# The output side of a SwiGLU on one core: where the low parts, the residual tiles and the last additions are made

## The chip, the cores and the metric

The kernel runs on one core of a Trainium2 chip. The metric is the device time of one execution in microseconds (us); the time given for a kernel is the median of its runs. The core's engines work side by side, each through a queue of its own, in order: TensorE (PE, with its weight loads PEld), VectorE (DVE), ScalarE (ACT), GpSimd (POOL) and SyncE (SP), which issues all DMAs of this kernel.

## The reference

One layer of a decoder trunk with 2048 tokens and 1024 channels, in float32. What matters here is its end:

```python
h = x * (1.0 + sc2) + sh2
gate, up = jnp.split(h @ w_ffn_in[l], 2, axis=-1)
f = (jax.nn.silu(gate) * up) @ w_ffn_out[l]
x = layer_norm(DEEPNORM_ALPHA * x + (1.0 + gt2) * f, ln2_g[l], ln2_b[l])
```

`w_ffn_out` has 2816 rows and 1024 columns. Ahead of this lie the input projection, a short convolution, an RWKV-7 time mixing and the output projection of the mixer with its own norm, which the change doesn't touch.

## The kernel before

Every large product is made in three matmuls of float32r operands: a float32 operand is split into a high part (a cast on ACT, line 232) and a low part (raw minus high, line 233, on an engine that the caller names), and TensorE adds high x high, low x high and high x low (lines 236 to 238, `mm3`). The two products of the SwiGLU also use the scheme with seven block products instead of eight (`PRODS`): the operands of a block product are sums or differences of blocks, made on DVE (line 988), then split.

The output side, the subject here, runs through 72 **steps**: seven products, each over 11 slices k of the hidden dimension. In the first six products a step serves both halves of the tokens: 2 halves x 4 tiles of 128 tokens x 3 matmuls, 24 of them. The last product is done for one half and then for the other, 12 matmuls a step. A product's eight PSUM banks (all that there are) collect over its 11 slices. Then `gather` (line 1007, DVE; copies on ACT in two products) adds each bank into the result tiles `c`, and the next product's first matmul on a bank waits for that.

`operands` makes what a step needs. For each half a tile `fr` is loaded (line 1235, four buffers), cast to `fh` on ACT and reduced to `fl` on DVE. For the weights one or two blocks `w` are loaded (line 1246), combined into `ws` on DVE (line 988, one buffer for even and one for odd k), cast to `oh` on ACT, and the low part `ol` is made by the engine that line 1274 passes to `combine`. The program asks for the operands of a step two steps ahead of its matmuls. The buffers (16 for `fh` and `fl`, four each for `oh` and `ol`) hold those of four steps.

Two more kinds of work go on beside the steps. `residuals` makes 32 tiles `r` of alpha * (normed x * g + b): a load of 128 x 512 values (line 1191) into buffers that the input side's operands used before, then a multiplication (line 1192) and an addition (line 1193). Sixteen are asked for in every second step of the first three products, the other sixteen one by one, each when `added` (line 1203, DVE) has used one up. `after` puts `added`, the statistics (line 1210, DVE) and `norm` into a list `later`, from which `do_later` takes one or two entries a step. `norm` works on a token tile: mean and variance (DVE), the root (POOL, lines 291 and 292), a scalar on DVE (line 293), then for each half row a scaling on ACT (line 1219), a multiplication on DVE (line 1220), an addition (line 1222; on DVE for the last four of 32, on POOL for the others) and the store.

The order on TensorE is the program's. On the other engines and on SP a planner sets the order: it keeps the program's order as priority, and in its own model of the time takes what is ready. So an engine's queue is fixed before the run, and on the chip an instruction whose input is late holds all behind it.

Of the kernel before, what the change touches and what calls it, by code (L numbers as in the profile page):

```python
# [14 lines left out]
ALU = mybir.AluOpType  # L15
# [7 lines left out]
S = 2048  # L23
# [10 lines left out]
HT = 1024  # L34
# [85 lines left out]
def kernel(  # L120
# [21 lines left out]
    act, dve, pool, pe = nc.scalar, nc.vector, nc.gpsimd, nc.tensor  # L142
# [87 lines left out]
    def split(hi, lo, raw, lo_eng=None):  # L230

        act.copy(out=hi, in_=raw)  # L232
        (lo_eng or pool).tensor_sub(lo, raw, hi)  # L233
# [13 lines left out]
    def f512(tag, name, bufs, dt=F32):  # L247
        return wp.tile([P, 512], dt, tag=tag, name=name, bufs=bufs)
# [38 lines left out]
    def norm_scale(st, u):  # L287
        mv = lnp.tile([P, 2], F32, tag="mv", name="mv" + u, bufs=2)
        dve.bn_aggr(out=mv, in_=st)
        rs = lnp.tile([P, 2], F32, tag="rs", name="rs" + u, bufs=2)  # L290
        pool.tensor_scalar(rs[:, 0:1], mv[:, 1:2], LN_EPS, None, ALU.add)
        pool.tensor_tensor(out=rs[:, 0:1], in0=rs[:, 0:1], in1=nhalf[:, 0:1], op=ALU.pow)  # L292
        dve.scalar_tensor_tensor(out=rs[:, 1:2], in0=mv[:, 0:1], scalar=-1.0, in1=rs[:, 0:1],  # L293
                                 op0=ALU.mult, op1=ALU.mult)
        return rs
# [9 lines left out]
    def out_proj(q, spawn, raws=None):  # L305
# [51 lines left out]
        for ns in ((0, 1), (2,), (3,), (4,), (5,), (6, 7)):  # L357
# [6 lines left out]
            for n, ps in zip(ns, pss):  # L364
                mt = lnp.tile([P, QT], F32, tag="mt", name=f"mt{q}_{n}", bufs=1)
                act.activation(mt, ps, AF.Identity, scale=gt1p[:, n:n + 1])
                spawn(add(n, mt))
        spawn(norm(), True)


# [614 lines left out]
    def plus_minus(out, blocks, terms, eng=None):  # L985

        a, b = terms
        (eng or dve).tensor_tensor(out=out, in0=blocks[a], in1=blocks[b.lstrip("-")],  # L988
                                   op=ALU.subtract if b[0] == "-" else ALU.add)

    def combine(blocks, terms, hi, lo, out, lo_eng):

        if len(terms) == 1:
            t = blocks[terms[0]]
        else:
            t = out()
            plus_minus(t, blocks, terms)
        split(hi, lo, t, lo_eng)
        return hi, lo
# [34 lines left out]
    with ExitStack() as ph2:  # L1034
# [128 lines left out]
        rw3 = []  # L1163
# [21 lines left out]
        def residuals():  # L1185

            for n, (b, half, t) in enumerate((b, half, t) for b in ("12", "11", "22", "21") for half in range(2)
                                             for t in range(4)):
                t0, ms = half * HT + (int(b[0]) - 1) * 512 + t * P, slice((int(b[1]) - 1) * 512, int(b[1]) * 512)
                r = fa.tile([P, 512], F32, tag=("h22", "h26")[n % 2], name=f"r{half}_{b}_{t}", bufs=8)  # L1190
                load(out=r, in_=xhd[t0:t0 + P, ms])
                pool.tensor_tensor(out=r, in0=r, in1=rw3[1][:, ms], op=ALU.mult)
                pool.tensor_tensor(out=r, in0=r, in1=rw3[2][:, ms], op=ALU.add)
                rs_made.append(r)
                yield

        stats = {}

        rs_made, rs_todo = collections.deque(), residuals()

        def added(half, b, t):
# [10 lines left out]
        def norm(c, half, a, t):  # L1212

            t0 = half * HT + (int(a) - 1) * 512 + t * P
            rs = norm_scale(stats[half, a, t], f"b{half}_{a}_{t}")
            for m in range(2):
                ms = slice(m * 512, (m + 1) * 512)
                z = c.pop((f"{a}{m + 1}", t))
                act.activation(z, z, AF.Identity, scale=rs[:, 0:1], bias=rs[:, 1:2])  # L1219
                dve.tensor_tensor(out=z, in0=z, in1=rw3[3][:, ms], op=ALU.mult)  # L1220
                end = m and half == S // HT - 1 and a == "2"
                (dve if end else pool).tensor_tensor(out=z, in0=z, in1=rw3[4][:, ms], op=ALU.add)  # L1222
                load(out=out[0, t0:t0 + P, ms], in_=z)


# [4 lines left out]
        def f_loads():  # L1230
            for halves, p, k in steps:
                i = PRODS[p][0]
                for half in halves:
                    f = fa.tile([P, 512], F32, tag="rawx", name=f"fr{half}_{i}_{k}", bufs=4)
                    load(out=f, in_=fd[half, i - 1, k])
                    yield f

        def w_loads():
            for halves, p, k in steps:
                if halves[0]:  # L1240
                    return
                blocks = {}
                for b in (b.lstrip("-") for b in PRODS[p][2]):
                    blocks[b] = fa.tile([P, 512], F32, tag="h25", name=f"w{p}_{b}_{k}", bufs=8)
                    ms = slice((int(b[1]) - 1) * 512, int(b[1]) * 512)
                    load(out=blocks[b], in_=wfs[FK * (int(b[0]) - 1) + k, :, ms])
                yield blocks

        def operands():
            fs, ws, blocks, kept = f_loads(), w_loads(), [], []  # L1250
            got = list(itertools.islice(fs, 2))
            for n, (halves, p, k) in enumerate(steps):
                i, _, terms = PRODS[p]
                F = {}
                for half in halves:
                    got += itertools.islice(fs, 1)
                    F[half] = [fa.tile([P, 512], F32R, tag=("h23", "h21")[n % 2], name=f"f{x}{half}_{i}_{k}", bufs=8)
                               for x in "hl"]
                    split(*F[half], got.pop(0), dve)
                if halves[0]:  # L1260
                    yield F, *kept.pop(0)
                    continue
                u = f"{i}_{k}"
                t = None
                if len(terms) == 2:
                    t = (lnp.tile([P, 512], F32, tag="mt", name="ws" + u, bufs=1) if k % 2 else
                         fa.tile([P, 512], F32, tag="us", name="ws" + u, bufs=1))
                if p == 6 and k < 8:
                    wh, wl = (fa.tile([P, 512], F32R, tag=tag, name=f"o{x}{u}", bufs=8)
                              for x, tag in (("h", "h22"), ("l", "h26")))  # L1270
                else:
                    wh, wl = (f512("w" + x, f"o{x}{u}", 4, F32R) for x in "hl")
                blocks += itertools.islice(ws, 3 - len(blocks))
                w = combine(blocks.pop(0), terms, wh, wl, lambda: t, pool)
                if p == 6:
                    kept.append(w)
                yield F, *w

        with tc.manual_schedule(engines={mybir.EngineType.PE}):
            todo3, got3 = operands(), []  # L1280

            run(ffn_in())
# [3 lines left out]
        def after(half, i, t):  # L1286

            then = {
                1: ((added, half, "12", t), (stat, c[half], half, "12", t)),
                4: ((added, half, "21", t),),  # L1290
                7: ((stat, c[half], half, "11", t), (norm, c[half], half, "1", t)),
                2: ((stat, c[half], half, "21", t),),
                6: ((stat, c[half], half, "22", t), (norm, c[half], half, "2", t)),
            }.get(i, ())
            return [functools.partial(*f) for f in then]
# [120 lines left out]
```

## Time and profile before

| | us |
|---|---|
| median of 3 runs | 2925.76 |
| lowest and highest run | 2925.40, 2932.94 |
| the profiled execution's own time | 2924.91 |
| its span, first to last instruction | 2922.7 |
| busy in the span: PE, DVE, ACT, POOL | 2680.6, 1921.0, 1095.7, 1412.7 |
| the output side: its first matmul, its last one | 2420.8, 2909.0 |

All rows come from the profiled execution. Times in a timeline are from the start of its span. A row that groups instructions gives line, engine, operation, output tile and inputs, the count, the busy time, the mean duration in ns, and then the idle time of that engine just ahead of them with what ended it. The stretches of a table by stretches were cut at the output side's matmuls: each time 264 of them (132 for the two parts of the last product) are one product. In such a table "PEclk" is the granted share of TensorE's full clock, 1.00 for 2.4 GHz and 0.50 for 1.2 GHz.

### The profile page before, as it was taken

The page shows a single profiled execution, that of the slowest core. Times are in us where ns is not written, and L with a number is a line of the kernel's source. Part 1 is how long each engine was busy: PE and PEld are TensorE (multiplying, and loading weights), DVE is VectorE, ACT ScalarE, POOL GpSimd, SP SyncE. Part 2 cuts the span into 40 slices and gives each one's busy share as a digit, 9 for nine tenths or more (in the row PEclk, how much of TensorE's full clock was granted, in tenths as well). Part 3 has the DMA queues.
Part 4 walks back from the last instruction along what each step waited for, and adds up shares of the span by engine and source line. Part 5 has one row for each costly group of instructions (what it writes and reads, how often), then busy time and mean ns, then how long its engine had stood idle before and what let it go on. Part 6 is the DMA issues. An engine that isn't in the chain of part 4 may idle for free. (4 is left out here: it accounts for less than half of the span.)

```text
span 2922.7 us, 50258 instructions
## 1 busy us (share of the span) xinstructions
PE 2680.6 (92%) x19232; PEld 2095.8 (72%) x19232; DVE 1921.0 (66%) x2964; ACT 1095.7 (37%) x1995; POOL 1412.7 (48%) x1104
## 2 busy tenths in 40 slices
PE   7879999999999999988599999988899998997998
PEld 6667777777777777767377888856678887776776
DVE  7354655556455565554674777798897778359597
ACT  4553433335433433434444433333233333332342
POOL 4665333323433333323544444458884448338383
PEclk7898999989999999999699999989999999998999
DMA  6443322234322222324353532235653337555563
GB/s 238 140 130 112 89 64 69 73 99 133 108 64 83 69 67 70 92 75 148 111 176 127 162 101 97 91 101 184 221 189 106 106 107 263 157 187 158 175 214 108
DMA packets 248344, 369.86 MB, mean 127 GB/s; under 512 B 58660, under 2 KB 81188, under 8 KB 248104
## 3 DMA queue, kind: packets, MB, share of 16 engines
q1 hardware_dynamic: 248104, 366.65, 39.5%
q8 instruction: 151, 2.47, 0.4%
q14 instruction: 89, 0.73, 0.1%
HBM read 278.99 MB, written 87.56 MB: 125 GB/s over the span
## 5 line engine op out<-in xcount | busy, mean ns | idle before, releaser
L236 PE MATMUL f<-uh,wh 128*128 128x512 f32 x1232 | 497.8, 404 | 31.9 <-ACT uh L232 27.4
L238 PE MATMUL f<-uh,wl 128*128 128x512 f32 x1232 | 496.2, 403 | 18.1 <-POOL wl L233 18.0
L237 PE MATMUL f<-ul,wh 128*128 128x512 f32 x1232 | 495.5, 402 | 11.8 <-DVE ul L233 7.2
L233 POOL TENSOR_TENSOR l<-r,h 128x512 fp32r<-128x512 f32 x201 | 265.6, 1324 | 438.4 <-ACT h L232 352.2
L233 POOL TENSOR_TENSOR wl<-ws,wh 128x512 fp32r<-128x512 f32 x220 | 316.1, 1438 | 295.5 <-ACT wh L232 264.1
L236 PEld LDWEIGHTS f<-uh,wh 128*128 128x128 f32 x1232 | 235.3, 191 | 92.6 <-ACT uh L232 31.8
L238 PEld LDWEIGHTS f<-uh,wl 128*128 128x128 f32 x1232 | 235.9, 191 | 83.4 <-POOL wl L233 27.9
L988 DVE TENSOR_TENSOR ws<-w,w 128x512 f32<-128x512 f32 x275 | 264.4, 984 | 43.6 <-POOL ol L233 24.6
L237 PEld LDWEIGHTS f<-ul,wh 128*128 128x128 f32 x1232 | 236.0, 192 | 72.4 <-DVE ul L233 9.4
L232 ACT CAST wh<-ws 128x512 fp32r<-128x512 f32 x220 | 136.7, 621 | 363.4 <-DVE ws L988 252.8
L236 PE MATMUL o<-oh,fh 128*128 128x512 f32 x616 | 249.5, 405 | 23.3 <-DVE c L1007 15.1
L1007 DVE TENSOR_TENSOR c<-f,c 128x512 f32<-128x512 f32 x264 | 181.1, 686 | 124.0 <-PE f L238 67.2
L237 PE MATMUL o<-ol,fh 128*128 128x512 f32 x616 | 247.9, 402 | 11.0 <-POOL ol L233 11.0
L238 PE MATMUL o<-oh,fl 128*128 128x512 f32 x616 | 247.8, 402 | 6.6 <-DVE fl L233 6.6
L233 DVE TENSOR_TENSOR fl<-fr,fh 128x512 fp32r<-128x512 f32 x154 | 149.7, 984 | 98.5 <-ACT fh L232 85.0
L232 ACT CAST h<-r 128x512 fp32r<-128x512 f32 x201 | 123.5, 616 | 214.3 <-PE d L270 156.7
L232 ACT CAST fh<-fr 128x512 fp32r<-128x512 f32 x154 | 94.9, 620 | 229.9 <-PE o L237 134.8
L233 POOL TENSOR_TENSOR lo<-ro,ho 128x512 fp32r<-128x512 f32 x64 | 84.7, 1328 | 199.1 <-ACT ho L232 144.3
L236 PEld LDWEIGHTS o<-oh,fh 128*128 128x128 f32 x616 | 119.4, 194 | 53.8 <-DVE c L1007 19.1
L233 POOL TENSOR_TENSOR wl<-w,wh 128x512 fp32r<-128x512 f32 x88 | 126.4, 1436 | 49.9 <-ACT wh L232 49.9
L237 PEld LDWEIGHTS o<-ol,fh 128*128 128x128 f32 x616 | 119.4, 194 | 40.7 <-POOL ol L233 14.4
L238 PEld LDWEIGHTS o<-oh,fl 128*128 128x128 f32 x616 | 119.4, 194 | 35.3 <-DVE fl L233 8.2
(499 smaller groups left out, 5898.2 us busy)
## 6 DMA issues: line engine op xcount, KB each, us to landing
r<-in_win_dram SPq DMA_DIRECT2D x201, 256.0 KB
w<-in_wfi_dram SPq DMA_DIRECT2D x176, 256.0 KB
fr<-fd SPq DMA_DIRECT2D x154, 256.0 KB
w<-wfs SPq DMA_DIRECT2D x132, 256.0 KB
fd<-fs SPq DMA_DIRECT2D x110, 256.0 KB
wm<-in_wmod_dram SPq DMA_DIRECT2D x72, 256.0 KB
ro<-in_wout_dram SPq DMA_DIRECT2D x64, 256.0 KB
fd<-th SPq DMA_DIRECT2D x44, 256.0 KB
```

Source lines behind the costliest of these rows:

```text
L232: act.copy(out=hi, in_=raw)
L233: (lo_eng or pool).tensor_sub(lo, raw, hi)
L236: pe.matmul(ps, lh, rh, start=start, stop=False)
L237: pe.matmul(ps, lh, rl, start=False, stop=False)
L238: pe.matmul(ps, ll, rh, start=False, stop=stop)
L988: (eng or dve).tensor_tensor(out=out, in0=blocks[a], in1=blocks[b.lstrip("-")], op=ALU.subtract if b[0] == "-" else ALU.add)
L1007: dve.tensor_tensor(out=c[b, t], in0=in0, in1=in1, op=op)
```

## The change

Three kinds of instruction go from POOL to DVE, all on the output side; nothing else is altered. They are the low parts `ol` of the weights (line 1274, 77 instructions), the two operations on each residual tile (lines 1192 and 1193, 64 instructions), and the addition that ends the norm (line 1222, 28 of 32, the other four being on DVE already). POOL keeps the two small operations of the norm's root (lines 291 and 292), and on the input side what it had.

```diff
@@ residuals
-                pool.tensor_tensor(out=r, in0=r, in1=rw3[1][:, ms], op=ALU.mult)
-                pool.tensor_tensor(out=r, in0=r, in1=rw3[2][:, ms], op=ALU.add)
+                dve.tensor_tensor(out=r, in0=r, in1=rw3[1][:, ms], op=ALU.mult)
+                dve.tensor_tensor(out=r, in0=r, in1=rw3[2][:, ms], op=ALU.add)
@@ norm
-                end = m and half == S // HT - 1 and a == "2"
-                (dve if end else pool).tensor_tensor(out=z, in0=z, in1=rw3[4][:, ms], op=ALU.add)
+                dve.tensor_tensor(out=z, in0=z, in1=rw3[4][:, ms], op=ALU.add)
@@ operands
-                w = combine(blocks.pop(0), terms, wh, wl, lambda: t, pool)
+                w = combine(blocks.pop(0), terms, wh, wl, lambda: t, dve)
```

## Rows read from the trace of the kernel before

**Rows 1.** The page's busy times: share of the span, number of instructions.

```profile
PE 2680.6 (92%) x19232; PEld 2095.8 (72%) x19232; DVE 1921.0 (66%) x2964; ACT 1095.7 (37%) x1995; POOL 1412.7 (48%) x1104
```

**Rows 2.** Busy time by stretches: products one to six, the last one's parts, the tail.

```profile
core 0: us, PE busy (x) PEld busy (x) DVE busy (x) ACT busy (x) POOL busy (x), PEclk, DMA share, GB/s
2420.82:2502.19 81.37, 67.44 (x275) 53.46 (x274) 62.77 (x45) 24.03 (x44) 70.17 (x45) 0.92 0.67 216
2502.19:2562.62 60.43, 60.43 (x266) 49.59 (x264) 22.94 (x34) 19.86 (x35) 15.30 (x11) 1.00 0.56 170
2562.62:2623.05 60.43, 60.43 (x266) 49.59 (x265) 31.96 (x47) 19.31 (x34) 16.80 (x12) 1.00 0.64 199
2623.05:2710.88 87.83, 69.84 (x266) 53.80 (x265) 84.97 (x77) 21.47 (x39) 70.32 (x43) 0.86 0.54 169
2710.88:2776.34 65.46, 63.52 (x265) 50.84 (x264) 34.17 (x55) 23.62 (x42) 20.56 (x19) 0.97 0.51 158
2776.34:2846.71 70.37, 65.02 (x265) 51.61 (x264) 66.14 (x68) 30.93 (x53) 59.15 (x44) 0.95 0.71 223
2846.71:2879.04 32.33, 30.67 (x134) 24.55 (x132) 24.05 (x42) 7.80 (x14) 2.27 (x4) 1.00 0.37 106
2879.04:2909.41 30.37, 30.37 (x133) 24.60 (x131) 25.57 (x38) 10.96 (x16) 21.25 (x21) 1.00 0.27 96
2909.41:2922.70 13.29, 0.00 (x1) 0.00 (x0) 8.31 (x12) 3.04 (x4) 4.79 (x5) 0.65 0.32 118
sum 501.88, PE 447.71 PEld 358.03 DVE 360.87 ACT 161.04 POOL 280.61; mean PE 49.75 PEld 39.78 DVE 40.10 ACT 17.89 POOL 31.18
```

**Rows 3.** POOL's groups of instructions by line on the output side.

```profile
L233 POOL TENSOR_TENSOR ol<-ws,oh 128x512 fp32r<-128x512 f32 x55 | 80.9, 1474 | 117.8 <-ACT oh L232 113.5 <-DMA fr<-fd 4.3
L1192 POOL TENSOR_TENSOR r<-r,rws 128x512 f32<-128x512 f32 x32 | 55.6, 1756 | 6.3 <-DMA r<-xhd 6.3
L1193 POOL TENSOR_TENSOR r<-r,rws 128x512 f32<-128x512 f32 x32 | 53.4, 1678 | 0.0
L1222 POOL TENSOR_TENSOR c<-c,b2r 128x512 f32<-128x512 f32 x28 | 43.0, 1549 | 9.4 <-DVE c L1220 9.4
L233 POOL TENSOR_TENSOR ol<-w,oh 128x512 fp32r<-128x512 f32 x22 | 32.6, 1485 | 44.7 <-ACT oh L232 44.7
```

**Rows 4.** DVE's low parts in the quiet stretch 2502 to 2613.

```profile
L233 DVE TENSOR_TENSOR fl<-fr,fh 128x512 fp32r<-128x512 f32 x42 | 30.2, 720 | 51.4 <-ACT fh L232 42.3 <-PE o L237 7.0 <-DMA w<-wfs 2.1
```

**Rows 5.** The same instructions in the crowded stretch 2424 to 2491.

```profile
L233 DVE TENSOR_TENSOR fl<-fr,fh 128x512 fp32r<-128x512 f32 x19 | 31.9, 1723 | 0.0
```

**Rows 6.** DVE's timeline (start, us): POOL idle in the first two rows, busy after.

```profile
2617.46 0.68 DVE L1007 TENSOR_TENSOR c<-o,c 128x512 f32<-128x512 f32 x1
2618.06 0.67 DVE L1007 TENSOR_TENSOR c<-c,c 128x512 f32<-128x512 f32 x1
...
2634.14 1.77 DVE L233 TENSOR_TENSOR fl<-fr,fh 128x512 fp32r<-128x512 f32 x1
2635.83 1.77 DVE L1203 TENSOR_TENSOR c<-c,r 128x512 f32<-128x512 f32 x1
```

**Rows 7.** What TensorE waited for, 2400 to the end: us, times, longest us.

```profile
PE o L236 <- DVE c L1007: 15.1, 8, 4.7
PE o L237 <- POOL ol L233: 11.0, 7, 4.8
PE o L236 <- ACT oh L232: 8.2, 2, 6.1
PE o L238 <- DVE fl L233: 6.6, 3, 3.7
```

**Rows 8.** One load's time to landing, in the chain that ended last.

```profile
2793.45 3.29 DMA fr<-fd
```

**Rows 9.** The last two additions of the norm, in the timeline.

```profile
2917.12 1.74 POOL L1222 TENSOR_TENSOR c<-c,b2r 128x512 f32<-128x512 f32 x1 [1.85 <-DVE c L1220]
2917.78 1.63 DVE L1222 TENSOR_TENSOR c<-c,b2r 128x512 f32<-128x512 f32 x1
```

## Prediction

> **What bounds the kernel now.** I first read the page's busy times: PE is busy for 92% of the span, DVE for 66%, POOL for 48% [rows 1]. That says TensorE sets the time, but not where it loses any. So I cut the output side into its products, 264 matmuls each, and read busy times for each stretch [rows 2]. The second and the third product show what TensorE can do: 60.43 us, PE busy throughout, the clock at 1.00. That is 0.229 us a matmul and 60.43 / 11 = 5.49 us a step. Against it the first product takes 81.4 us, the fourth 87.8, the fifth 65.5, the sixth 70.4, and the first part of the last 32.3 instead of 30.2. In the first product 9 of the 275 matmuls belong to the input side (others count 266), 9 x 0.229 = 2.1 us. The excess is then 21.0 - 2.1 = 18.9, 27.4, 5.0, 9.9 and 2.1 us: **63.3 us** in all, and part of it is the clock, granted at 0.92, 0.86, 0.97 and 0.95 in those four products.
>
> The bad products are those in which POOL is busy: 70.2, 70.3 and 59.2 us in the first, fourth and sixth, 15 to 21 in the others. What TensorE waits for there [rows 7] is the gathering of a bank on DVE (15.1 us), `ol` from POOL (11.0), `oh` (8.2, the cast behind a late `ws`) and `fl` from DVE (6.6). Together they are 40.9 us; the other 22 us of the excess are the lower clock around the stalls and short gaps.
>
> Why are they late? The same instruction, `fl` on DVE, takes 0.72 us in the quiet stretch and 1.72 us in the crowded one [rows 4, 5]. The timeline shows the cause as far as a timeline can: while POOL stands idle, DVE starts an instruction every 0.60 us; while POOL works on SBUF tiles, DVE's with two SBUF inputs start 1.69 us apart [rows 6], and POOL's mean is 1.47 to 1.76 us [rows 3]. Side by side the two engines finish two instructions in about 1.7 us. DVE by itself finishes two in 1.2 us. So a second engine adds no throughput here; it takes some.
>
> **The change, part by part.** 77 `ol`, 64 residual operations and 28 additions leave POOL, 169 instructions that cost it 80.9 + 32.6 + 55.6 + 53.4 + 43.0 = 265.5 us [rows 3]. On DVE I price one at the pitch with POOL idle, 0.60 us [rows 6]: 101 us. No row shows these three operations on DVE alone, but `fl` is the same subtraction on the same shape; its mean of 0.72 us [rows 4], which has some shared ones in it, is the upper price, 122 us. In return DVE's own instructions fall from up to 1.7 us to 0.6. I count what each product then asks of DVE: the instructions of both engines, less the tiny ones of the norm, times 0.60, against TensorE's 60.4 us [rows 2]:
> - first product: 45 + 45 = 90, 54 us
> - second and third: 45 and 59, 27 and 35 us
> - fourth: 77 + 43 = 120, 72 us
> - fifth: 74 less 12 tiny ones, 37 us
> - sixth: 112 less 20 tiny ones, 55 us
> - last: 105 less some 28 tiny ones, 46 us
>
> Only the fourth asks more than it has, by 12 us. Operands may be made up to three steps ahead, 16 us, and the fifth product has 60.4 - 37 = 23 us to spare, so a delay of 12 us of `added` and residual work can be put off, as far as the queue's order puts it behind the operands. The program asks for a step's operands ahead of that step's `later` entries, which speaks for it.
>
> What is late next, product by product, with what I leave of each excess:
> - First, 18.9: the last gathers of the input side hold the first banks and end when the last matmul of that side allows; 17 instructions at 0.6 us in their way instead of 13 at up to 1.8. The stalls on `ol` near its end go. I leave 6 (2 to 11), a gain of **13** (8 to 17).
> - Fourth, 27.4: DVE's 72 us stay above TensorE's. With full cover nothing is left, with none 12 and a clock dip. I leave 5 (0 to 13), a gain of **22.5** (14 to 27).
> - Fifth, 5.0: the wait at its end for a gather and a clock dip. A gain of **3.5** (1 to 5).
> - Sixth, 9.9: here each step gets a `norm` entry, five full DVE instructions beside the four of the operands, 9 x 0.60 = 5.4 us against 5.49. That is tight. A gain of **6** (1 to 9).
> - Last, 2.1: a gain of **1** (0 to 2).
> - Tail of 13.3 us [rows 2]: the last two additions, 1.74 and 1.63 us side by side [rows 9], become two of 0.6 us in turn; against that, DVE has one or two more instructions ahead of the last gather. **0.5** (-1 to +1).
>
> The second and the third product lose nothing, since 27 and 35 us of DVE work in 60.4 leave room; without that room each `ol` would come 0.6 us later per instruction ahead of it. DVE's queue gets two new waits: `ol` behind ACT's cast, and line 1192 behind the load of `r`. Queued behind them are `fl`, `ws` and the gathers, and TensorE waits for those. POOL waited only once for a load of `r`, 6.3 us of 32 loads [rows 3]. The first I price at nothing, because the planner can put another instruction into the 0.6 us of the cast; without that cover it is 77 x 0.6 = 46 us of DVE time, spread over products that mostly have it. SP's queue loses its waits for POOL and gets as many for DVE; its order around them may change, and I price that at nothing, between -2 and +2 us.
>
> Two rules speak against this sum. POOL is busy for 48% of the span and DVE for 66% [rows 1], so work goes from the emptier engine to the fuller one. The Trainium skill, *Perfetto Trace Analysis*, "Identifying the Most-Contended Engine", takes occupancy as a fair measure of how close Vector and GPSIMD are to their limits. By it DVE would be overfilled; that is the third rival. And DVE's starts lie 0.60 us apart although an instruction is shown for 0.67 to 0.68 us [rows 6]. The Trainium skill, *VectorE: DVE Perf Modes*, "The DRAIN you can't avoid", has the next one start only when the pipeline is empty. By 0.68 us a start the fourth product would ask 82 us of DVE instead of 72, and the whole would come out some 10 us later; the row decides.
>
> **The sum.** 13 + 22.5 + 3.5 + 6 + 1 + 0.5 = 46.5 us. The profiled execution's time is 2924.9 us (span 2922.7), 0.9 below the median of the runs, so the sum holds for both: 2925.8 - 46.5 = **2879 us**. The best ends add up to 61 us, the worst to 23: 2865 to 2903 us.
>
> **Rivals.**
> 1. *DVE becomes the bound in its crowded products.* The planner puts residual or norm work ahead of operands, and one queue now carries everything. Then the first product keeps 12 of its excess, the fourth 20, the sixth all: a gain of 6.9 + 7.4 + 3.5 + 1 = 19 us, **2907 us**. For it speaks the fourth product's 72 us, against it the look-ahead of 16 us. Chance 0.12.
> 2. *Slower, through the loads of the residual tiles.* In DVE's queue line 1192 waits for its landing and everything behind it waits too. If each of the 32 waits for w, the first product asks 54 + 16w of DVE and the fourth 72 + 16w. With what the other parts gain (11), the change is even at 18.9 + 27.4 + 11 = (54 + 16w - 60.4) + (72 + 16w - 60.4), w = 1.6 us. At a whole landing time of 3.3 us [rows 8] it loses 32 x (3.3 - 1.6) = 54 us, **2980 us**. Against it: one wait in 32 on POOL [rows 3], whose queue ran late. Chance 0.04.
> 3. *The durations go along.* If 1.5 to 1.7 us were the price of the work itself, DVE would need 361 + 265 = 626 us in a stretch of 502 [rows 2, 3]: 124 us more, **3050 us**. The 0.60 us starts speak against it [rows 6]. Chance 0.01.
> 4. *All stalls go*, more than 61 us gained: about **2862 us**. Every product would run like the second. Chance 0.05.
>
> The change could also fail to do what it says, if the planner's other order on ACT and SP cancels it; that is within the first rival.
>
> **How the numbers follow.** My forecast of 2865 to 2903 has a chance of 0.78. For 8 in 10 the range goes to 2864 and to 2906, into the first rival. Some 0.3%, or 9 us, is what a measurement of this kernel can tell from no change. All of the forecast and of rival 4 is faster by more, and 0.08 of the 0.12 of rival 1: 0.91. Rival 1 leaves 0.04 within it. Slower is 0.05, rivals 2 and 3.
>
> **What would show it.** Every `fl`, `ws`, `ol` and `r` on DVE should have a mean near 0.65 us on the output side, and DVE's busy time there should not rise above its 361 us although it has 169 instructions more. The first and the fourth product should take 62 to 75 us, with the clock near 1.00. The second and the third should stay at 60.4. The forecast is wrong if DVE's instructions stay above 1 us with POOL idle, if DVE shows idle time ended by the load of `r`, or if TensorE waits for `fl` or the gathers as long as now.

## The result and the profile after

| | before | after |
|---|---|---|
| median of 4 runs, us | 2925.58 | 2879.55 |
| lowest and highest run | 2924.19, 2932.94 | 2877.66, 2885.85 |
| the profiled execution's own time | 2924.91 | 2881.27 |
| its span | 2922.7 | 2879.5 |
| output side, first matmul to last | 488.6 | 444.8 |
| from there to the end | 13.3 | 11.5 |

The ratio of the times is 0.9847, with a 95% interval of 0.9834 to 0.9861: 46.0 us less by the medians, 41 to 49 by the interval (0.0139 and 0.0166 of 2925.6), where 46.5 were forecast.

First the table by stretches, cut at the same matmuls as [rows 2]: products one to six, the two parts of the last, the tail.

```profile
2423.20:2491.23 68.03, 64.95 (x276) 52.47 (x274) 55.78 (x92) 26.41 (x47) 0.47 (x1) 0.97 0.77 264
2491.23:2551.66 60.43, 60.43 (x266) 49.58 (x265) 28.85 (x45) 19.80 (x35) 0.00 (x0) 1.00 0.54 170
2551.66:2612.09 60.43, 60.43 (x266) 49.59 (x265) 36.58 (x58) 19.30 (x34) 0.00 (x0) 1.00 0.65 199
2612.09:2686.22 74.13, 64.26 (x266) 51.27 (x265) 73.58 (x123) 23.42 (x41) 0.00 (x0) 0.95 0.64 207
2686.22:2746.76 60.54, 60.54 (x266) 49.50 (x264) 37.13 (x64) 22.86 (x39) 2.89 (x6) 1.00 0.52 166
2746.76:2807.59 60.83, 60.73 (x266) 49.50 (x264) 59.13 (x109) 32.34 (x54) 6.10 (x10) 1.00 0.77 260
2807.59:2837.64 30.05, 30.05 (x134) 24.79 (x133) 20.77 (x37) 7.27 (x13) 1.00 (x3) 1.00 0.35 105
2837.64:2868.01 30.37, 30.36 (x133) 24.58 (x131) 24.07 (x49) 11.35 (x17) 6.42 (x12) 1.00 0.27 96
2868.01:2879.50 11.49, 0.00 (x0) 0.00 (x0) 6.61 (x13) 2.67 (x4) 1.02 (x2) 0.66 0.37 137
sum 456.30, PE 431.75 PEld 351.29 DVE 342.52 ACT 165.43 POOL 17.90; mean PE 47.97 PEld 39.03 DVE 38.06 ACT 18.38 POOL 1.99
```

The columns are those of [rows 2]. Products five and six and the last one now run at TensorE's own pace, the clock at 1.00. The first went from 81.4 to 68.0 us, the fourth from 87.8 to 74.1: these two are what is left. The sum row has the surprise that was forecast: DVE is busy for 342.5 us, less than the 360.9 before, with 169 instructions more. By product the gains are 13.3, 13.7, 4.9, 9.5 and 2.3 us, and 1.8 in the tail, 45.6 in all (the differences to [rows 2]; 0.1 is rounding). The output side began at 2423.2, not 2420.8, so the profiled spans differ by 43.2 only.

That start is not the change's doing. The order of work on DVE and ACT up to there is the same, and the 2.4 us are there already at the first matmul of the SwiGLU's input product (1405.6 us before, 1408.7 after). Among the profiled executions of this study with an unaltered input side that matmul lies between 1398.7 and 1408.7 us, and the output side's first one between 2413.5 and 2423.2. So below I compare the length of the output side, or of one product, and take whole times only as medians.

DVE's groups on the output side, answering to [rows 3 to 5] (L1221 is line 1222 of the kernel before):

```profile
L233 DVE TENSOR_TENSOR fl<-fr,fh 128x512 fp32r<-128x512 f32 x150 | 103.6, 693 | 94.1 <-ACT fh L232 85.8 <-PE o L237 8.2
L233 DVE TENSOR_TENSOR ol<-ws,oh 128x512 fp32r<-128x512 f32 x55 | 38.5, 705 | 0.7 <-ACT oh L232 0.7
L1193 DVE TENSOR_TENSOR r<-r,rws 128x512 f32<-128x512 f32 x32 | 21.7, 705 | 0.0
L1192 DVE TENSOR_TENSOR r<-r,rws 128x512 f32<-128x512 f32 x32 | 21.6, 700 | 0.0
L1221 DVE TENSOR_TENSOR c<-c,b2r 128x512 f32<-128x512 f32 x28 | 19.1, 688 | 0.0
```

Each moved instruction is shown for about 0.70 us, and so is `fl`, crowded or not. Ahead of the residual operations DVE never sat idle for a load: their idle time is 0.0. What TensorE still waits for, answering to [rows 7]:

```profile
PE o L237 <- DVE ol L233: 8.9, 4, 6.1
PE o L236 <- DVE c L1007: 4.1, 2, 2.4
```

13.0 us instead of 40.9. The longest wait, 6.1 us in the fourth product, is for an `ol`, and DVE's timeline shows why it was late (x2 and x3 are two and three in a row):

```profile
2644.40 0.70 DVE L988 TENSOR_TENSOR ws<-w,w 128x512 f32<-128x512 f32 x1
2644.99 0.71 DVE L233 TENSOR_TENSOR fl<-fr,fh 128x512 fp32r<-128x512 f32 x1
2645.59 1.32 DVE L1192 TENSOR_TENSOR r<-r,rws 128x512 f32<-128x512 f32 x2
2646.80 0.71 DVE L988 TENSOR_TENSOR ws<-w,w 128x512 f32<-128x512 f32 x1
2647.40 1.31 DVE L1203 TENSOR_TENSOR c<-c,r 128x512 f32<-128x512 f32 x2
2648.61 0.71 DVE L233 TENSOR_TENSOR fl<-fr,fh 128x512 fp32r<-128x512 f32 x1
2649.21 0.71 DVE L1203 TENSOR_TENSOR c<-c,r 128x512 f32<-128x512 f32 x1
2649.81 1.31 DVE L1193 TENSOR_TENSOR r<-r,rws 128x512 f32<-128x512 f32 x2
2651.01 0.71 DVE L233 TENSOR_TENSOR fl<-fr,fh 128x512 fp32r<-128x512 f32 x1
2651.62 1.91 DVE L1203 TENSOR_TENSOR c<-c,r 128x512 f32<-128x512 f32 x3
2653.42 0.71 DVE L233 TENSOR_TENSOR ol<-ws,oh 128x512 fp32r<-128x512 f32 x1
```

Starts are 0.60 us apart, without a gap. Between the first `ws` and its `ol`, nine microseconds later, stand ten instructions of residual work.

### The profile page after: what moved, and what is told of

It is laid out like the page before. It is cut to its first block, busy times and chain, and to the rows that moved or that the text cites. A ratio compares the mean times of both kernels' runs of the same rounds, so it can differ in the third digit from the quotient of the medians.

```text
span 2879.5 us, 50206 instructions
## 1 busy us (share of the span) xinstructions
PE 2660.8 (92%) x19232; PEld 2082.8 (72%) x19232; DVE 1898.7 (66%) x3133; ACT 1098.7 (38%) x1995; POOL 1148.7 (40%) x935
## 4 chain that ended last, share of the span: by engine, by line
PE 40%; DVE 5%; DMA 4%; POOL 2%; issue 1%; ACT 0%; SPq 0%; POOLq 0%; DVEq 0%; ACTq 0%
PE f L238 8%; PE f L237 8%; PE f L236 8%; PE o L237 4%; PE o L238 4%; PE o L236 4%; PE do L270 3%; DMA wf<-in_wfo_dram 2%; DMA wfs<-wf 2%; POOL wf L1172 1%; DVE c L1007 1%; DVE ws L988 1%; DMA b<-h2d 0%; DVE ul L233 0%; POOL wl L233 0%
## 5 line engine op out<-in xcount | busy, mean ns | idle before, releaser
L233 POOL TENSOR_TENSOR l<-r,h 128x512 fp32r<-128x512 f32 x201 | 265.2, 1321 | 444.8 <-ACT h L232 359.5
L238 PEld LDWEIGHTS f<-uh,wl 128*128 128x128 f32 x1232 | 234.8, 191 | 85.6 <-POOL wl L233 30.5
L988 DVE TENSOR_TENSOR ws<-w,w 128x512 f32<-128x512 f32 x275 | 242.8, 907 | 18.0 <-DMA w<-wfs 7.4
L236 PE MATMUL o<-oh,fh 128*128 128x512 f32 x616 | 242.1, 393 | 4.2 <-DVE c L1007 4.1
L233 DVE TENSOR_TENSOR fl<-fr,fh 128x512 fp32r<-128x512 f32 x154 | 106.2, 693 | 94.1 <-ACT fh L232 85.8
```

The source lines that it names most:

```text
L236: pe.matmul(ps, lh, rh, start=start, stop=False)
L238: pe.matmul(ps, ll, rh, start=False, stop=stop)
```

## The experiments

Theory A: an instruction of DVE with two SBUF inputs and one of POOL slow each other down, so what counts is how long both work side by side. Theory B: DVE's pace does not matter; a moved instruction takes 0.7 us instead of 1.5, and `ol` leaves POOL's queue. A second question is what the fourth product still loses.

### One part of the change alone

Three kernels each make one of the three edits of the change and leave out the other two.

```diff
 only_residuals
-                pool.tensor_tensor(out=r, in0=r, in1=rw3[1][:, ms], op=ALU.mult)
-                pool.tensor_tensor(out=r, in0=r, in1=rw3[2][:, ms], op=ALU.add)
+                dve.tensor_tensor(out=r, in0=r, in1=rw3[1][:, ms], op=ALU.mult)
+                dve.tensor_tensor(out=r, in0=r, in1=rw3[2][:, ms], op=ALU.add)
 only_low_parts
-                w = combine(blocks.pop(0), terms, wh, wl, lambda: t, pool)
+                w = combine(blocks.pop(0), terms, wh, wl, lambda: t, dve)
 only_norm_add
-                (dve if end else pool).tensor_tensor(out=z, in0=z, in1=rw3[4][:, ms], op=ALU.add)
+                dve.tensor_tensor(out=z, in0=z, in1=rw3[4][:, ms], op=ALU.add)
```

> Of the change only the 64 residual operations go to DVE; the low parts ol and the last additions of the norm stay on POOL. Theory A (an instruction of DVE with two SBUF inputs and one of POOL slow each other down, so what counts is how long both work side by side): the residual work is POOL's long stretch in products one and four, so most of their gain comes by it alone: 22 to 32 us faster than before (2894 to 2904 us), product six as slow as before (about 70 us), fl on DVE near 0.75 us in the first product. Theory B (the gain is that a moved instruction takes 0.7 us instead of 1.5 and ol leaves POOL's queue; DVE's own pace does not matter): residual tiles were never waited for, so only ol's freer queue on POOL helps, 11 us of waits: 5 to 12 us faster (2914 to 2921 us).

> Of the change only the 77 low parts ol go to DVE; residual tiles and norm additions stay on POOL. Theory A: POOL still works for 109 us on residual tiles beside DVE, now with more instructions on the slowed DVE: between 8 us faster and 8 us slower than before (2918 to 2934 us); product four stays above 82 us, fl in it above 1.1 us. Theory B: ol no longer queues behind residual tiles and takes half as long, so the 11 us of waits for it and the clock behind them come back: 15 to 30 us faster (2896 to 2911 us).

> Of the change only the 28 additions that end the norm go to DVE. Theory A: product six, where POOL made 14 of them, falls from 70.4 to 61 to 65 us and the tail loses 1 to 2 us; products one and four as before: 6 to 11 us faster (2915 to 2920 us). Theory B: nobody on TensorE waits for these additions, only the stores do; 0 to 2 us faster, all of it in the tail (2924 to 2926 us).

Measured: 2895.73 us with the residual operations alone (ratio to before 0.9911, 0.9894 to 0.9927), 2908.70 with the low parts alone (0.9952, 0.9937 to 0.9967), 2917.68 with the norm's additions alone (0.9979, 0.9968 to 0.9990). The output sides are 458.1, 473.5 and 483.0 us long, 30.5, 15.1 and 5.6 less than before. The parts add up to 51.2 us, all together gave 43.8, so they share some of it.

The tables by stretches, each with products one, four and six: first the residual operations alone, then the low parts alone, then the additions alone.

```profile
2418.79:2488.70 69.91, 65.81 (x275) 53.13 (x274) 56.19 (x78) 24.33 (x44) 29.39 (x13) 0.95 0.76 254
2609.55:2679.22 69.67, 63.81 (x265) 51.47 (x264) 68.51 (x105) 23.10 (x40) 28.05 (x11) 0.95 0.63 198
...
2743.13:2814.83 71.70, 65.05 (x265) 51.12 (x264) 67.68 (x70) 31.54 (x54) 59.25 (x44) 0.95 0.69 220
```

```profile
2422.51:2496.55 74.04, 67.27 (x276) 53.35 (x275) 67.80 (x57) 23.08 (x43) 56.56 (x32) 0.95 0.70 234
2617.40:2710.31 92.91, 66.60 (x266) 52.68 (x265) 86.12 (x96) 23.63 (x41) 48.63 (x31) 0.83 0.52 167
...
2770.73:2832.87 62.14, 60.99 (x266) 49.43 (x265) 60.32 (x87) 31.86 (x54) 31.39 (x26) 1.00 0.75 249
```

```profile
2422.14:2503.71 81.57, 67.60 (x275) 53.69 (x274) 62.77 (x45) 24.58 (x45) 70.20 (x45) 0.92 0.66 216
2624.57:2712.36 87.79, 69.65 (x266) 53.67 (x264) 84.71 (x75) 21.00 (x37) 69.84 (x43) 0.86 0.53 169
...
2777.52:2844.67 67.15, 63.27 (x266) 50.53 (x265) 62.83 (x88) 31.61 (x54) 40.23 (x29) 0.97 0.74 235
```

The residual operations came out as A had them and B had not, product six no faster at 71.7 us; only `fl` in the first product, 0.83 us in the mean, stayed above the 0.75 expected. The low parts did not: A's 2918 to 2934 us missed, B's 2896 to 2911 held. In the fourth product A was right: with POOL still 48.6 us on residual tiles it got worse, 87.8 to 92.9 us, since `ol` now waits in the slowed queue (TensorE waited for it once for 17.1 us); `fl` there has a mean of 0.95 us, not the 1.1 expected. What I had not counted is that `ol` leaves POOL also in the first and the sixth product, where that shortens the time side by side (POOL 70.2 to 56.6 and 59.2 to 31.4 us); they gained 7.3 and 8.2 us. The norm's additions brought the forecast total, but product six only fell to 67.2, not to 65: POOL still made 19 `ol` there. These three do not tell A from B cleanly.

### POOL busy again, for nobody

The changed kernel, and beside each residual tile POOL works on a scratch tile that nobody else reads. The two kernels differ in what POOL does: in the first it reads SBUF, in the second it only writes. The lines that set up the two scratch tiles are left out here.

```diff
                 dve.tensor_tensor(out=r, in0=r, in1=rw3[2][:, ms], op=ALU.add)
+                act.copy(out=scr[0][:, 0:1], in_=r[:, 0:1])
 pool_reads
+                pool.tensor_tensor(out=scr[0], in0=scr[0], in1=scr[1], op=ALU.mult)
+                pool.tensor_tensor(out=scr[0], in0=scr[0], in1=scr[1], op=ALU.mult)
 pool_writes
+                for _ in range(4):
+                    pool.memset(scr[0], 1.0)
```

> The changed kernel, and for each of the 32 residual tiles POOL makes two multiplications of two scratch tiles of 128 x 512 that nobody reads; a one-column copy on ACT (behind the residual tile) sets when they may start. 64 two-input instructions on POOL, some 85 to 110 us of it, come back beside DVE in products one and four without any work that TensorE needs. Theory A (two-input instructions of DVE and POOL slow each other): DVE's instructions in those products go to 1.0 to 1.7 us again and 20 to 45 us come back, against the changed kernel's 2880 (2900 to 2925 us). Theory B (only the moved instruction's own time and its queue count): POOL's work is off every path, within 4 us of the changed kernel (2876 to 2884 us).

> As the kernel with POOL's scratch multiplications, but POOL fills a scratch tile of 128 x 512 four times for each residual tile: it is busy and writes SBUF, but reads none. Theory A in the narrow form (the slowing is for POOL's reads against DVE's second SBUF input): as the changed kernel, 2876 to 2886 us, DVE's instructions at 0.7 us. Theory A in the wide form (any work of POOL on SBUF slows DVE): 10 to 45 us slower than the changed kernel. Theory B: 2876 to 2884 us.

Measured: 2929.67 us with the reads, which is before's time again and a little more (1.0014, 1.0004 to 1.0024), and 5 us above A's range; 2871.61 us with the writes (0.9813, 0.9793 to 0.9833), 4 us below the range that the narrow form and B gave it. The output sides are 496.7 and 446.4 us, against 444.8 of the changed kernel. By the profiles the second kernel's lower time is its earlier start, since its output side began at 2414.5 and is 1.6 us longer. The fourth product, by engine: `fl` on DVE and what POOL did, first with reads, then with writes.

```profile
L233 DVE TENSOR_TENSOR fl<-fr,fh 128x512 fp32r<-128x512 f32 x20 | 21.2, 1061 | 6.2 <-ACT fh L232 6.2
...
L1198 POOL TENSOR_TENSOR scr<-scr,scr 128x512 f32<-128x512 f32 x16 | 41.6, 2600 | 147.2 <-ACT scr L1197 147.2
L1199 POOL TENSOR_TENSOR scr<-scr,scr 128x512 f32<-128x512 f32 x16 | 25.0, 1565 | 1.3
```

```profile
L233 DVE TENSOR_TENSOR fl<-fr,fh 128x512 fp32r<-128x512 f32 x22 | 15.0, 685 | 2.1 <-ACT fh L232 2.1
...
L1199 POOL MEMSET scr<- 128x512 f32 x64 | 33.7, 526 | 158.5 <-ACT scr L1197 155.8
```

DVE's timeline in the kernel with reads, where a burst of POOL's multiplications takes hold (in this kernel lines 1195 and 1196 are the residual operations and 1216 the statistics; POOL's own spans are rough):

```profile
2642.29 0.68 DVE L1195 TENSOR_TENSOR r<-r,rws 128x512 f32<-128x512 f32 x1
2642.89 0.68 DVE L1216 BATCH_NORM_STATS2 kst<-c 128x6 f32<-128x512 f32 x1
2643.49 1.18 DVE L1196 TENSOR_TENSOR r<-r,rws 128x512 f32<-128x512 f32 x1
2644.60 1.74 DVE L233 TENSOR_TENSOR fl<-fr,fh 128x512 fp32r<-128x512 f32 x1
2646.26 1.75 DVE L1195 TENSOR_TENSOR r<-r,rws 128x512 f32<-128x512 f32 x1
```

No work of the layer uses the scratch tile, and yet the whole gain is gone. The test has one flaw: the copy on ACT that releases POOL waits itself until POOL has done the burst before, and casts stand behind it in ACT's queue. The output side of this kernel, and two of its waits:

```profile
2413.53:2910.20 496.67, 442.85 (x1859) 357.12 (x1857) 389.07 (x568) 165.52 (x304) 150.00 (x94) 0.95 0.55 176
...
ACT scr L1197 <- POOL scr L1199: 73.6, 20, 17.9
...
PE o L237 <- DVE ol L233: 35.3, 6, 10.0
```

Through ACT, TensorE lost 8.4 us on one `oh`, whose `ws` had been done since 2683.6 (the wait ended at 2697.1), and DVE stood idle once for 3.3 and once for 6.2 us until an `fh` came; with the writes the same copy waited 16.8 us in all. That part of the loss is not DVE's pace. But for the same instructions DVE was busy for 389.1 us, 53 more than in the changed kernel (335.9), and TensorE waited 35.3 us for `ol` from it instead of 8.9. Two of these waits, 6.8 us ending at 2651.4 and 10.0 us ending at 2675.2, come out of a stretch from 2620 on in which DVE was never idle. So B, by which DVE's pace does not matter, falls; how the 52 us of the output side divide between ACT's waits and DVE's pace was not measured.

The mean of 2600 ns hides that the two engines do not always take turns. One multiplication was held for 18.9 us:

```profile
2426.24 18.92 POOL L1198 TENSOR_TENSOR scr<-scr,scr 128x512 f32<-128x512 f32 x1 [13.48 <-ACT scr L1197]
```

Within it DVE started 29 instructions with two SBUF inputs, 0.60 us apart. POOL went on only when DVE paused, at 2444.0, and behind that pause DVE's instructions started 1.67 us apart. From 2671.9 on it happened again, for 16.4 us and 25 instructions. So DVE is slowed where POOL's reads come in between its instructions, not wherever POOL has one waiting.

With POOL busy for 33.7 us but reading nothing, `fl` stays at 0.69 us: A holds in its narrow form, POOL's reads against DVE's second SBUF input. The Trainium skill, *SBUF — State Buffer*, "Who interferes with whom", has just that rule: a DVE instruction with two SBUF inputs contends with a GpSimd instruction that reads SBUF, not with one that only writes it. The two runs agree with it.

### What the fourth product still loses

It has 122 full DVE instructions, 73 us, in TensorE's 60.4. Four kernels ask whether the amount or the order is to blame. The first leaves the residual tiles' scale and shift out; the second slows the list of later work; the third pins that work behind the operands (`behind(dve)`, which the kernel has, puts what is issued in its block after the last DVE instruction issued so far, here the `ol` of the step two ahead); the fourth moves it to the next product.

```diff
 no_residual_ops
-                dve.tensor_tensor(out=r, in0=r, in1=rw3[1][:, ms], op=ALU.mult)
-                dve.tensor_tensor(out=r, in0=r, in1=rw3[2][:, ms], op=ALU.add)
 pace16
-                do_later(2 if len(later) > 8 else 1)
+                do_later(2 if len(later) > 16 else 1)
 hold_later
+                with behind(dve) if p == 3 else ExitStack():
+                    do_later(2 if len(later) > 8 else 1)
 spread (and in `added` the line next(rs_todo, None) goes)
+                with behind(dve) if p in (3, 4) else ExitStack():
+                    do_later(2 if len(later) > 16 else 1)
+                    if n > 32 and (n % 2 or n > 48):
+                        next(rs_todo, None)
```

> The changed kernel without the two residual operations: the loaded tiles are added as they are, so the residual's scale and shift are left out and the result differs. Asks what the 13.7 us are that product four still loses. Theory 'demand' (DVE has 73 us of work for TensorE's 60.4): without 32 of 122 instructions there, 19 us less, product four takes 60.4 to 62 us and product one loses 1 to 3 us less than now: 12 to 18 us faster than the changed kernel (2862 to 2868 us). Rival 'boundary' (the loss is the wait for the gathers at the product's start and the clock behind it): product four stays at 70 us or more, 0 to 5 us faster.

> The changed kernel, with two entries of the list of later work taken in a step only while more than 16 wait, not more than 8, so some of the additions and residual tiles move from product four into product five, which has 23 us to spare on DVE. Theory 'demand in the wrong place' (product four's 13.7 us are DVE work put ahead of the operands in its queue): product four falls to 61 to 68 us and product five stays under 62, 5 to 13 us faster than the changed kernel (2867 to 2875 us). Rival: the planner makes the residual tiles as early as their loads allow whatever the list's pace: within 4 us of the changed kernel (2876 to 2884 us).

> The changed kernel; in product four alone, every DVE instruction of the list of later work (additions of the residual tiles, the residual operations, statistics) must stand in DVE's queue behind the low part ol of the step two ahead. No work is added or taken out. Theory 'order' (what product four still loses, 13.7 us, is residual work that stands ahead of ol in one queue; DVE has 23 us to spare in product five): product four takes 61 to 66 us, product five up to 62, output side 8 to 13 us shorter than the changed kernel's 444.7 us, 2867 to 2873 us. Theory 'demand' (73 us of work in 60.4 cannot fit, wherever it stands): product four or five shows the loss again, output side within 4 us of 444.7.

> The changed kernel, its work unaltered, but the second half of the residual tiles is asked for over products four and five, one in two steps, not with each addition, the list of later work is taken at two a step only while more than 16 wait, and in both products all of this stands in DVE's queue behind the low part ol of the step two ahead. That should take about 30 of the 122 instructions out of product four's time and into product five's. Theory 'demand' (product four loses because DVE has 73 us of work in it, whatever the order): with some 92 instructions, 55 us, it takes 60.4 to 65 us, product five stays under 62.5; output side 430 to 437 us, 5 to 12 us shorter than the changed kernel's 444.7. Rival 'boundary and order' (the stalls come from the gathers and from a planner that runs ahead): product four stays above 70 us.

The fourth product in the four kernels, in this order; for the last one the fifth and the sixth too:

```profile
2604.91:2667.92 63.01, 60.98 (x265) 49.43 (x264) 55.94 (x93) 23.29 (x41) 0.00 (x0) 1.00 0.75 244
```

```profile
2602.05:2675.57 73.52, 64.01 (x266) 51.04 (x265) 72.97 (x122) 23.37 (x41) 0.00 (x0) 0.95 0.66 210
```

```profile
2609.05:2682.71 73.66, 64.90 (x265) 52.09 (x264) 72.92 (x123) 23.32 (x41) 0.00 (x0) 0.93 0.67 212
```

```profile
2607.79:2668.22 60.43, 60.43 (x266) 49.58 (x264) 55.65 (x93) 23.25 (x41) 0.00 (x0) 1.00 0.79 257
2668.22:2728.65 60.43, 60.43 (x266) 49.58 (x265) 52.40 (x88) 19.95 (x35) 1.41 (x4) 1.00 0.55 168
2728.65:2789.07 60.42, 60.42 (x265) 49.58 (x264) 58.75 (x111) 32.99 (x55) 8.66 (x13) 1.00 0.79 264
```

Without the residual operations it has 93 instructions and takes 63.0 us (output side 429.6, whole time 2860.65 us): 1.0 us above and 1.4 us below what "demand" has, far from "boundary". The slower list changed nothing in it: the planner put the same 122 instructions there, 73.5 us; the first product was 3.5 us shorter, though DVE's queue is the same one in it, so that is a difference between executions. My theory for that kernel fell, and its whole time of 2871.05 us, inside that theory's range, came from an earlier start of the output side (2416.7 us) and from that first product. Pinning the order alone gave 73.7 us as well, with the stalls later in the product (2878.34 us, output side 441.9): "demand" held, "order" fell. Spreading left 93 in product four and put 88 in product five, and both take TensorE's own 60.4 us, with the clock at 1.00. The output side is 427.1 us, 17.7 less than the changed kernel's and 3 less than the least expected, the whole 2865.99 us (0.9795, 0.9778 to 0.9812). So the amount of DVE work within the product is the cause of nearly all of it. The last 2.6 us, 63.0 against 60.4 with 93 instructions each, may be the order, which only the second of these two kernels pins; no kernel separates the two.

### Further in the same direction

On the input side DVE and POOL work side by side too. Here the low parts of weights and moving operands and the scaling of the output weights go to DVE.

```diff
 input_side
-                U[half, i, k] = combine(raws, terms, hi, lo, sums, (dve, pool)[n % 2])
+                U[half, i, k] = combine(raws, terms, hi, lo, sums, dve)
...
-                                      lambda: temp(f"ws{u}_{i}"), pool)
+                                      lambda: temp(f"ws{u}_{i}"), dve)
...
-                    pool.tensor_tensor(out=w, in0=w, in1=rw3[0][:, ms], op=ALU.mult)
+                    dve.tensor_tensor(out=w, in0=w, in1=rw3[0][:, ms], op=ALU.mult)
```

> The changed kernel, and on the input side of the SwiGLU too the low parts of weights and moving operands and the scaling of the output weights go from POOL to DVE. Between 1900 and 2200 us TensorE loses about 50 us while both engines are busy (DVE 44 to 48 and POOL 31 to 46 of 50 us). Theory A (side by side costs): 74 instructions per 50 us cost DVE 44 us alone, so most of it fits: 15 to 35 us faster than the changed kernel (2845 to 2865 us). Theory B: DVE, fuller, becomes late: 0 to 30 us slower (2880 to 2910 us).

> The input side's work on DVE as well, and product four's later work held behind the operands: the sum of the two if they are independent, since they lie in different stretches. Theory A with 'order': 2835 to 2857 us. Theory B with 'demand': 2880 to 2910 us.

> The same spreading, with the input side's low parts and weight scaling on DVE as well. The two lie in different stretches and should add: 2845 to 2855 us, the output side as long as in the kernel with the spreading alone.

Measured: 2859.53 us (0.9775, 0.9761 to 0.9788), some 20 us under the changed kernel, as A has it. Of that the input side itself gave 14: from its first matmul to the output side's first one are 1000.5 us in the profile, and 1014.5 in the changed kernel's; alone that is 1 us under A's 15 to 35. The rest is the first product, 64.3 us here, and the earlier start. Together with the pinned order it is 2859.06 us, the same, since the pinning gave nothing; that missed its range. With the spreading it is **2844.70 us** (0.9720, 0.9707 to 0.9733), 0.3 us below the least expected, 82 us less than before and the fastest of all; its input side takes 1000.2 us and its output side 427.1, so the two do add.

## Why the prediction was right, and where it was not

The forecast was 2879 us and 2879.55 were measured. That it is so close is partly luck, as the terms show: one of them was too large by 9 us, the others together too small by 8, and four of the six lie outside their own ranges.

- **Bound.** TensorE's pace of 5.49 us a step and the 63.3 us of excess over it: right. The kernel with the spreading runs every product but the first at this pace, and no product ran faster.
- **The price of an instruction.** 0.60 us each when DVE works alone: right, and the term that mattered most. 122 instructions took 73.6 us of DVE in the fourth product. At 0.68 us a start it would have been 83 us. By the Trainium skill, *VectorE: DVE Perf Modes*, "The DRAIN you can't avoid", the next instruction starts when the pipeline is empty, but the same paragraph excepts one that is not held, which starts earlier. I had read the rule without its exception; the starts 0.60 us apart agree with the exception, and so do not speak against the page. Rival 3, durations that go along, is out: DVE's busy time fell.
- **First product:** 13 forecast, 13.3 measured. With the same queue there, other kernels of the study needed 64.5 to 65.1 us, so 3 us of it vary between executions. In the changed kernel's profile TensorE waited 2.4 us for a gather there, and the granted clock fell to a mean of 0.62 from 2435.2 to 2439.2 (0.50 is the lower of its two levels); with the spreading that wait was 1.5 us and the clock stayed at 1.00.
- **Fourth product:** 22.5 forecast, 13.7 measured, just outside the 14 to 27. I had the demand right, 72 us for 60.4, and the bound too: with no cover, 12 us and a clock dip are left. The step that failed is the one that put the delay off, "a delay of 12 us of `added` and residual work can be put off, as far as the queue's order puts it behind the operands". The planner had 31 of the 32 residual operations of the second half and 26 of the 32 additions in this product, and only three additions later, and the kernel with the pinned order shows that standing behind the operands does not help while they stay. Only moving them to the fifth product, whose 23 us I had counted as free, did.
- **Fifth, sixth, last, tail:** 3.5, 6, 1 and 0.5 forecast, 4.9, 9.5, 2.3 and 1.8 measured, the last three above their ranges. In the sixth 5.4 us of DVE work a step against 5.49 is enough; I had called it tight and left 4 us. Why the last product and the tail gained more was not looked into.
- **Rival 1** (DVE becomes the bound) came true in part, in the fourth product alone, which kept 13.7 us where it had 20. **Rival 2** (loads of the residual tiles) did not: no idle time on DVE ended by them. **Rival 4**, all stalls gone, is what the spreading nearly reaches.
- The new wait of `ol` for ACT's cast cost 0.7 + 2.3 us of DVE's idle time over the whole output side. I had priced it at nothing.

What stays open: why the work before the SwiGLU ends up to 10 us earlier or later from one profiled execution to another; how much of the loss in the kernel with POOL's reads came through ACT; and part of the 2 us that the first product still loses in the kernel with the spreading (64.6 us, less ten matmuls of the input side, 2.3, and 60.4), of which 1.5 us are the one wait for a gather.

## What to carry to other kernels

Two engines that hold each other up when both read SBUF have to be planned as one resource: price an instruction on either from a stretch in which the other is idle, and ask whether one alone does both shares sooner. Then count the work of the fuller engine within each stage, not over the whole, because a queue that is full in one stage delays what stands in it even where the next stage has room. And before trusting a look-ahead or an order to hide work, move the work.

## What the runs showed of the hardware

POOL's multiplications on SBUF tiles slowed DVE's two-input instructions from 0.60 to about 1.67 us from start to start where the two took turns, its memsets (0.53 us each) not at all. As long as DVE's two-input instructions followed one another without a gap, POOL's multiplication was held instead, for up to 18.9 us. A DVE instruction with one input in PSUM kept its 0.68 us beside POOL. In the fourth product of the kernel with the low parts alone, gathers from a PSUM bank have a mean of 681 ns, `fl` 946, and the gathers' additions of two SBUF tiles 1410:

```profile
L233 DVE TENSOR_TENSOR fl<-fr,fh 128x512 fp32r<-128x512 f32 x22 | 20.7, 946 | 4.4 <-ACT fh L232 4.4
...
L1007 DVE TENSOR_TENSOR c<-c,c 128x512 f32<-128x512 f32 x6 | 8.5, 1410 | 0.0
L1007 DVE TENSOR_TENSOR c<-o,c 128x512 f32<-128x512 f32 x10 | 6.8, 681 | 0.0
```

Only three of these ten gathers lay within a POOL instruction, but in the kernel before 14 of 47 did, with a mean of 682 ns. So it is the second input from SBUF that is held up: beside the gathers POOL's work cost DVE nothing.
